# The largest expert goes last, and the final norm's steps are queued later beside it

## Chip, core and metric

The kernel runs on one core of one Trainium2 chip. The metric is the device time of one execution in microseconds, as the median of several runs. Engines are named as the profile names them: PE is TensorE, DVE is VectorE, ACT is ScalarE, POOL is GpSimd, SP is SyncE. Each engine works through its own instructions in the order in which they were queued.

## What is computed

One layer of a diffusion backbone over 1024 latent tokens of width 1024 with 256 context tokens: token mixers first, then a mixture of 16 experts, then an RMSNorm over the result. Only the last two matter here. Each token goes to two experts of one group, and each expert is a gated product of width 1536:

```python
def expert_block(args):
    xb, e = args
    return (jax.nn.silu(xb @ w_g[e]) * (xb @ w_u[e])) @ w_d[e]
...
y = y_blk[dest].reshape(n_tok, TOP_K, d) * weight[..., None].astype(h.dtype)
return jnp.sum(y, axis=1)
...
x = x + gt2 * y[:n_lat].reshape(bsz, seq, d)
...
return rms_norm(x, g_final)
```

## The kernel before

The last 1055 us or so of the span are a loop over 16 **slots**, one expert each. The order of the experts is a table of ranks by the number of their tokens: `RANK[slot]` is the rank of the expert that a slot works on (0 is expert 0, whose weights can be fetched before the counts are known; 1 is the largest of the others, 15 the smallest). `UNITS[slot]` follows from it: every expert has 128 token rows (the A rows, gathered into `xa`), rank 1 has two further **units** of 32 rows, ranks 2 to 9 have one, the others none (the B rows, gathered into `xb`; one unit is laid over the 128 partitions as four column quarters of 256). So there are slots of no unit, of one unit, and one of two units.

An expert's weights come in 18 **pages** of 1 MB, 12 of `w_gu` (gate and up) and 6 of `w_d` (down), which SP loads (`load`, L1179) into a ring of ten buffers named `raw` and `praw`. ACT copies a page to a rounded high part (`hl`, L1192), DVE subtracts it for a low part (L1193); three `hl` buffers exist. `block_a` (L1372) then makes 12 products of 128x512 for a page with the A rows, six for each column half (`pa`); `block_b` (L1385) uses the pages as they were loaded for the B rows (`pb`). A slot has three gate/up chunks of four pages (c0, c1, c2), whose results go through SiLU on ACT (`sa`, L1592; `sb_` for B rows), a product on DVE (L1593), and transposes on PE (`aat`, `abt`, copied to `aah`, `aal` and `abT`), and a down part of six pages, in two halves of three. With units, `block_b` of a chunk or a half comes ahead of its `block_a`. At a slot's end DVE scales the result (`ya`, L1632; `yb`, L1625) and POOL adds its rows to `x1_d` in DRAM by an indirect DMA (L1430).

The last slot also makes the final norm. `TAIL` says at which chunk which step is issued: `f0` to `f3` (`fetched`, L1510) read 256 rows of `x1_d` each, `f0` into a tile of its own (`fx`), the others into buffers of the page ring; `n0` to `n3` (`normed`) square 128 rows at a time with a running sum on ACT (`fq`, L1517), make 1/sqrt by 12 small DVE steps (`rstd`, L215 to L223), scale the rows by it and by g_final, and write them to `out` (L1525). `NE` says with which engine a half of such rows is scaled: "S" is a scaling on ACT (L1521) and a product on POOL (L1522), "V" one instruction on DVE (L1524). The rows of the last expert are written again behind that, from `xg`: the rows of `x1_d` gathered earlier plus `ya`, squared (L1635), normed (L1639), and scattered into `out` (L1534).

```python
TAIL = dict(g0=["f0", "f1"], g2=["g", "n0", "n1", "f2"], d0=["f3"], d2=["n2", "n3"])
RANK = (0, 1, 10, 2, 11, 3, 12, 4, 13, 5, 14, 6, 7, 8, 9, 15)
```

`g0` to `g2` are called behind c0 to c2, `d0` and `d2` behind a down page. The framework's scheduler queues an instruction where its own priorities put it, which can be ahead of the place at which it is written.

Of the kernel before, what the change touches and what calls it, by code (L numbers as in the profile page):

```python
# [21 lines left out]
E = 16  # L22
# [22 lines left out]
FQB = 1  # L45
EPX = 1
FOLD = 2
NE = ["SS", "SV", "SV", "VV"]
TAIL = dict(g0=["f0", "f1"], g2=["g", "n0", "n1", "f2"], d0=["f3"], d2=["n2", "n3"])
QW = 260  # L50


RANK = (0, 1, 10, 2, 11, 3, 12, 4, 13, 5, 14, 6, 7, 8, 9, 15)
UNITS = tuple(0 if r == 0 else 2 if r == 1 else 1 if r < 10 else 0 for r in RANK)
C_C, C_CC, C_G1, C_BB, C_BM, C_GLA, C_LNG = 0, 8, 16, 24, 40, 56, 64
N_COLS = 72
# [105 lines left out]
def body(tc, A, out):  # L162
# [1148 lines left out]
    def places():  # L1311

        X = mybir.AxisListType.X
        sq = [128, 16, 16]
        key = ep_.tile([128, 16], F32, name="key")
        V.scalar_tensor_tensor(key, cf, 16.0, ks[:, 3], op0=ALU.mult, op1=ALU.add)
        w = ep_.tile(sq, F32, name="w16")
        V.tensor_tensor(w, key[:, None, :].to_broadcast(sq), key[:, :, None].to_broadcast(sq), op=ALU.is_gt)
        rank = ep_.tile([128, 16], F32, name="rank")
        V.tensor_reduce(rank, w, axis=X, op=ALU.add)  # L1320
        sel = ep_.tile(sq, F32, name="sel")
        V.tensor_tensor(sel, ks[:, 0, :, None].to_broadcast(sq), rank[:, None, :].to_broadcast(sq), op=ALU.is_equal)
# [23 lines left out]
        V.tensor_reduce(rank[0:1, 0:1], more[:, 0], axis=X, op=ALU.max)  # L1346
        V.tensor_copy(cnt[:, 3:4], rank[0:1, 0:1])
# [15 lines left out]
        SP.dma_start(g2B[32 * g:32 * g + 32],  # L1363
                     mod_d[6 + g // 2:7 + g // 2, 256 * (g % 2):256 * (g % 2) + 256].to_broadcast([32, 256]))

    def block_a(acc, st, k0, pg, start, stop):

        wh, wl = pg
        for k in range(2):
            for n, (x, w) in enumerate(((0, wh), (0, wl), (1, wh))):  # L1370
                for h in range(2):
                    end = PE.matmul(acc[h], st[x][:, k0 + k, :], w[:, k, 512 * h:512 * h + 512],  # L1372
                                    start=start and (k, n) == (0, 0), stop=stop and (k, n) == (1, 2))
        return end

    def block_b(n, acc, st, k0, pgs, first, last):
# [127 lines left out]
    def rows_of(a, i):  # L1504
        return a[256 * i:256 * i + 256].rearrange("(j p) c -> p j c", j=2)

    def fetched(i, pool=None):

        fx[i] = (pool or ep_).tile([128, 2, D], F32, name="fx") if pool or i < EPX else page_tile([128, 2, D])
        GP.dma_start(fx[i], rows_of(x1_d, i))  # L1510

    def normed(i, gf):
        x1 = fx[i]
        sq = ep_.tile([128, D], BF16, name="fq", bufs=FQB)
        ss = ep_.tile([128, 2, 2], F32, name="fs", bufs=2)
        for j in range(2):
            SC.activation(sq, x1[:, j], AF.Square, accum_out=ss[:, 0, j:j + 1])  # L1517
        rstd(ss[:, 1], ss[:, 0], 2, 1.0 / D, ep_)
        for j in range(2):
            if NE[i][j] == "S":  # L1520
                SC.activation(x1[:, j], x1[:, j], AF.Copy, scale=ss[:, 1, j:j + 1])  # L1521
                GP.tensor_mul(x1[:, j], x1[:, j], gf)  # L1522
            else:
                V.scalar_tensor_tensor(x1[:, j], x1[:, j], ss[:, 1, j:j + 1], gf, op0=ALU.mult, op1=ALU.mult)  # L1524
        GP.dma_start(rows_of(out, i), x1)  # L1525

    def quarters(r0, tile_):
        a = A["rows"]
# [11 lines left out]
    def tail(at):  # L1540
        nonlocal gf, xg
        for n in TAIL.get(at, ()):
            if n == "g":
                gf = ep_.tile([128, D], F32, name="gf")
                bcast("rows", 2 * D, D, gf)
                xg = ep_.tile([128, D], F32, name="xg", tag="xa", bufs=1)
                gather(xg, x1_d, tkA[:, E - 1:E])
            elif n[0] == "f":
                fetched(int(n[1]))
            else:  # L1550
                normed(int(n[1]), gf)

    gf = xg = None
    wAB = prep_a(0, *first_xa, ch0), []
    before = []

# [13 lines left out]
    for e in range(E):  # L1570
        U = UNITS[e]
        left = None
        for c in range(3):
# [15 lines left out]
            for h in range(2):  # L1589
                sa = ep_.tile([128, 2, 128], F32, name="sa", bufs=4)  # L1590
                pv = pa[h].rearrange("p (g u n) -> p g u n", g=2, u=2)
                SC.activation(sa, pv[:, :, 0], AF.Silu)  # L1592
                mul = V.tensor_mul(sa, sa, pv[:, :, 1])  # L1593
                sas.append(sa)
            left = c, sas, sb_ if U else None, U
# [4 lines left out]
                    if e == 0:  # L1600
                        places()
            if e + 1 == E:
                tail(f"g{c}")
            elif c == 1:
                nxt = gathered(e + 1)
        pa, pb = [pt(f"pa{h}", "pa", 4) for h in range(2)], pt("pb", "pb", 2) if U else None
        for i in range(0, 6, 3):
# [4 lines left out]
            if i == 3 and e + 1 < E:  # L1612
                wAB = prep(e + 1, *nxt)
            for k in range(i, i + 3):
                end = block_a(pa, AA, 2 * k, page(), k == 0, k == 5)
                if k == 0 and not U:
                    turned_a(*left, end)
                if e + 1 == E and k % 2:
                    tail(f"d{k - 1}")
        ya = ep_.tile([128, D], F32, name="ya", bufs=2)  # L1620
        yb = ep_.tile([128, 2, 256], F32, name="yb", bufs=2)
        last = e + 1 == E
        wA, wB = wAB_
        for j in range(U):
            V.scalar_tensor_tensor(yb[:, j], pb[:, 256 * j:256 * j + 256], wB[j], g2B, op0=ALU.mult, op1=ALU.mult)  # L1625
        if last:

            sl = ep_.tile([128, 8], F32, name="sl")
            sq = ep_.tile([128, D], BF16, name="fq", bufs=FQB)
# [6 lines left out]
        if last:  # L1636
            V.tensor_add(sl[:, 6:7], sl[:, 4:5], sl[:, 5:6])
            rstd(sl[:, 7:8], sl[:, 6:7], 1, 1.0 / D, ep_)
            V.scalar_tensor_tensor(xg, xg, sl[:, 7:8], gf, op0=ALU.mult, op1=ALU.mult)  # L1639
            put_out(xg, tkA[:, e:e + 1], out, S - 1)  # L1640
        if last:
            break
        st = [put(ya, tkA[:, e:e + 1], x1_d, (), before)]
# [9 lines left out]
    any_more = nc.values_load(cnt[0:1, 3:4], min_val=0, max_val=1)  # L1653
    with tc.If(any_more > 0):
        put(ya, tkA[:, E - 1:E], x1_d)
        flat = more.rearrange("o b e -> o (b e)")
# [7 lines left out]
        np_ = tc.alloc_tile_pool(name="np", bufs=1)  # L1664
        for t in range(4):
            fetched(t, np_)
            normed(t, gf)
        np_.release()
    ep_.release()
# [17 lines left out]
```

## Time and profile before

| | |
|---|---|
| median of 3 runs (lowest to highest) | 2233.47 us (2231.7 to 2234.19) |
| the profiled execution | 2234.38 us, its span 2232.6 us |
| PE busy | 2152.0 us, 96% of the span |
| DVE, ACT, POOL busy | 63%, 47%, 10% |
| HBM | 236 GB/s over the span |

The span runs from the first to the last instruction in the profile of one execution, and the time holds 1.8 us more than it. Matmuls are pipelined, so a busy PE is only an engine that never waits for more than a moment. A busy share over the whole span says little about the last slot, which is 4% of it.

### The profile page before, as it was taken

The numbers are of one execution on the slowest core, as the hardware profiler recorded it, in microseconds if no ns is written. First come the engines' busy times: TensorE is split into PE (matmuls) and PEld (weight loads), VectorE is DVE, ScalarE is ACT, GpSimd is POOL, SyncE is SP. The second block draws the span as 40 slices with busy tenths as digits, with TensorE's granted clock in tenths as the row PEclk, the third lists the DMA queues.
The fourth block names the chain that finished last, engine by engine and source line by source line (L and its number), as shares of the span: only waits on it lengthen the run. The fifth ranks groups of instructions, "written<-read, shape, count | busy, mean of one in ns | idle before, by whom it ended". The sixth has DMA issues, their size and how long they took to land. (4 is left out here: it accounts for less than half of the span.)

```text
span 2232.6 us, 36046 instructions
## 1 busy us (share of the span) xinstructions
PE 2152.0 (96%) x14286; PEld 1788.1 (80%) x14287; DVE 1414.7 (63%) x2127; ACT 1057.8 (47%) x1327; POOL 212.6 (10%) x174
## 2 busy tenths in 40 slices
PE   8999999999999999999978999999999999999975
PEld 6999898888889978888966777787878787777753
DVE  5754214847672354344888568787978787777766
ACT  3412114635542234233226456676767666556554
POOL 0011000000000000000343111100101010100031
PEclk9999999999999999999989999999999999999988
DMA  7576433556652175545648779898989898877774
GB/s 297 180 226 178 157 131 105 178 186 198 219 201 72 38 258 202 191 135 205 189 185 304 269 261 368 301 368 306 364 301 377 302 350 337 290 277 295 283 245 160
DMA packets 141791, 529.63 MB, mean 237 GB/s; under 512 B 17126, under 2 KB 57758, under 8 KB 94512
## 3 DMA queue, kind: packets, MB, share of 16 engines
q1 hardware_dynamic: 119584, 467.84, 57.3%
q0 software_dynamic: 20880, 55.16, 8.6%
q10 hardware_dynamic: 1152, 4.26, 0.5%
q8 instruction: 114, 1.87, 0.3%
q14 instruction: 61, 0.50, 0.1%
HBM read 457.09 MB, written 70.31 MB: 236 GB/s over the span
## 5 line engine op out<-in xcount | busy, mean ns | idle before, releaser
L1193 DVE TENSOR_TENSOR hl<-praw,hl 128x2048 fp32r<-128x2048 f32 x174 | 400.3, 2303 | 130.5 <-ACT hl L1192 125.7
L1372 PE MATMUL pa<-hl,xah 128*128 128x512 f32 x1536 | 421.1, 395 | 19.8 <-ACT hl L1192 13.4
L1192 ACT ACTIVATE hl<-praw 128x2048 fp32r<-128x2048 f32 x174 | 333.6, 1919 | 151.7 <-PE pa L1372 150.5
L1372 PEld LDWEIGHTS pa<-hl,xah 128*128 128x128 f32 x1536 | 286.4, 189 | 85.2 <-ACT hl L1192 13.8
L1193 DVE TENSOR_TENSOR hl<-raw,hl 128x2048 fp32r<-128x2048 f32 x114 | 260.7, 2290 | 86.7 <-ACT hl L1192 83.1
L1192 ACT ACTIVATE hl<-raw 128x2048 fp32r<-128x2048 f32 x114 | 218.8, 1919 | 100.3 <-PE pa L1372 95.5
L1372 PE MATMUL pa<-hl,xal 128*128 128x512 f32 x768 | 238.2, 391 | 0.0
L256 PE MATMUL mm<-wh,hxh 128*128 128x256 f32 (+1 forms) x768 | 218.9, 285 | 1.0 <-DVE vv L285 0.7
L1372 PE MATMUL pa<-hl,aah 128*128 128x512 f32 x768 | 212.4, 398 | 6.5 <-DVE hl L1193 5.0
L256 PE MATMUL mm<-wl,hxh 128*128 128x256 f32 (+1 forms) x768 | 217.7, 283 | 0.0
L256 PE MATMUL mm<-wh,hxl 128*128 128x256 f32 (+1 forms) x768 | 217.3, 283 | 0.0
L256 PE MATMUL mm<-hxh,wh 128*128 128x512 f32 x448 | 176.4, 394 | 0.0
L256 PE MATMUL mm<-hxh,wl 128*128 128x512 f32 x448 | 176.3, 394 | 0.0
L256 PE MATMUL mm<-hxl,wh 128*128 128x512 f32 x448 | 176.3, 393 | 0.0
L1372 PEld LDWEIGHTS pa<-hl,aah 128*128 128x128 f32 x768 | 142.8, 190 | 35.6 <-DVE hl L1193 5.9
L1372 PEld LDWEIGHTS pa<-hl,xal 128*128 128x128 f32 x768 | 145.0, 189 | 31.1
L256 PEld LDWEIGHTS mm<-wh,hxh 128*128 128x128 f32 x768 | 146.5, 191 | 1.8 <-DVE vv L285 0.9
L256 PEld LDWEIGHTS mm<-wl,hxh 128*128 128x128 f32 x768 | 146.6, 191 | 0.0
L238 DVE TENSOR_TENSOR wl<-wraw,wh 128x2048 fp32r<-128x2048 f32 (+1 forms) x36 | 82.7, 2298 | 100.7 <-ACT wh L237 100.6
L256 PEld LDWEIGHTS mm<-wh,hxl 128*128 128x128 f32 x768 | 146.3, 190 | 0.0
L1372 PE MATMUL pa<-hl,aal 128*128 128x512 f32 x384 | 120.2, 393 | 0.0
L237 ACT ACTIVATE wh<-wraw 128x2048 fp32r<-128x2048 f32 (+1 forms) x36 | 69.0, 1918 | 65.9 <-PE mm L256 60.7
(489 smaller groups left out, 3588.2 us busy)
## 6 DMA issues: line engine op xcount, KB each, us to landing
praw<-in_w_gu_dram SPq DMA_DIRECT2D x116, 1024.0 KB, 6.2
raw<-in_w_gu_dram SPq DMA_DIRECT2D x76, 1024.0 KB, 6.3
praw<-in_w_d_dram SPq DMA_DIRECT2D x58, 1024.0 KB, 7.2
raw<-in_w_d_dram SPq DMA_DIRECT2D x38, 1024.0 KB, 7.0
wraw<-in_w_in_dram SPq DMA_DIRECT2D x24, 1024.0 KB, 4.7
wraw<-in_w_mod_dram SPq DMA_DIRECT2D x18, 1024.0 KB, 5.9
vb<-v_d POOLq DMA_DIRECT2D x16, 1024.0 KB, 6.8
xt<-in_x_dram SPq DMA_DIRECT2D x16, 512.0 KB, 5.5
```

Of the source, the lines that this page charges most:

```text
L237: SC.activation(wh[:, :n], raw[:, :n], AF.Copy)
L238: V.tensor_sub(wl[:, :n], raw[:, :n], wh[:, :n].bitcast(F32))
L256: end = PE.matmul(acc, Wst[a](k), Wmv[b](k), start=n == 0, stop=n == tot - 1)
L1192: SC.activation(hl[:, 0, :], raw, AF.Copy)
L1193: V.tensor_sub(hl[:, 1, :], raw, hl[:, 0, :].bitcast(F32))
L1372: end = PE.matmul(acc[h], st[x][:, k0 + k, :], w[:, k, 512 * h:512 * h + 512], start=start and (k, n) == (0, 0), stop=stop and (k, n) == ( ...
```

## The change

- `RANK` puts the largest expert (two units) into slot 15 and the smallest into slot 12. Slot 1 now has one unit. The list of units by slot changes from 0 2 0 1 0 1 0 1 0 1 0 1 1 1 1 0 to 0 1 0 1 0 1 0 1 0 1 0 1 0 1 1 2.
- `TAIL` fetches `f0` and `f1` behind c0, and `f2` and `f3` behind c1; `n0` is issued behind c1 and `n2` behind c2. `normed` now takes four times 128 rows at once (two fetches), squares them on ACT, runs one `rstd` for four columns, and scales all of them on DVE; nothing of it is left on POOL but the DMAs. `issue_after` holds its instructions back until the chunk's SiLU and product have been queued.
- The units of the last expert are normed beside the down part: `xq` (their rows of `x1_d`), squares, a product `sums` with the constant `k32` on PE which adds the four quarters of a row, an `rstd`, and two scatters into `out`.
- `block_a` of the very last page makes all products of the first column half, then those of the second.

```diff
-NE = ["SS", "SV", "SV", "VV"]
-TAIL = dict(g0=["f0", "f1"], g2=["g", "n0", "n1", "f2"], d0=["f3"], d2=["n2", "n3"])
+TAIL = dict(g0=["f0", "f1"], g1=["g", "f2", "f3", "n0"], g2=["n2"])
...
-RANK = (0, 1, 10, 2, 11, 3, 12, 4, 13, 5, 14, 6, 7, 8, 9, 15)
+RANK = (0, 2, 10, 3, 11, 4, 12, 5, 13, 6, 14, 7, 15, 8, 9, 1)
...
-        for k in range(2):
-            for n, (x, w) in enumerate(((0, wh), (0, wl), (1, wh))):
-                for h in range(2):
+        steps = [(h, k, n) for k in range(2) for n in range(3) for h in range(2)]
+        for h, k, n in sorted(steps) if in_turn else steps:
...
     def normed(i, gf):
+        ss = ep_.tile([128, 2, 4], F32, name="fs", bufs=2)
+        tiles = [fx[i + n // 2][:, n % 2] for n in range(4)]
+        for n, x1 in enumerate(tiles):
+            SC.activation(sq, x1, AF.Square, accum_out=ss[:, 0, n:n + 1])
+        rstd(ss[:, 1], ss[:, 0], 4, 1.0 / D, ep_)
+        for n, x1 in enumerate(tiles):
+            V.scalar_tensor_tensor(x1, x1, ss[:, 1, n:n + 1], gf, op0=ALU.mult, op1=ALU.mult)
+            if n % 2:
+                GP.dma_start(rows_of(out, i + n // 2), fx[i + n // 2])
...
+                with tc.issue_after(act.ins), tc.issue_after(mul.ins):
+                    normed(int(n[1]), gf)
...
+            if i == 3 and last:
+                sl = ep_.tile([128, 16], F32, name="sl")
+                sq = ep_.tile([128, D], BF16, name="fq", bufs=FQB)
+                for j in range(U):
+                    V.scalar_tensor_tensor(yb[:, j], pb[:, 256 * j:256 * j + 256], wB[j], g2B, op0=ALU.mult,
+                                           op1=ALU.mult)
+                    V.tensor_add(xq[:, j], xq[:, j], yb[:, j])
+                    SC.activation(sq[:, 256 * j:256 * j + 256], xq[:, j], AF.Square, accum_out=sl[:, 8 + j:9 + j])
             for k in range(i, i + 3):
-                end = block_a(pa, AA, 2 * k, page(), k == 0, k == 5)
+                end = block_a(pa, AA, 2 * k, page(), k == 0, k == 5, last and k == 5)
...
+                if last and k == 4:
+                    p = pt("sums", "pt", 2)
+                    with tc.issue_after(end.ins):
+                        PE.matmul(p[:, 0:U], k32, sl[:, 8:8 + U], start=True, stop=True)
+                    rstd(sl[:, 10:10 + U], p[:, 0:U], U, 1.0 / D, ep_)
+                    ends = []
+                    for j in range(U):
+                        V.scalar_tensor_tensor(xq[:, j], xq[:, j], sl[:, 10 + j:11 + j], gq, op0=ALU.mult,
+                                               op1=ALU.mult)
+                        ends.append(put_out(xq[:, j], tkB[:, j, e:e + 1], out_quarter, 4 * S - 1, ends))
```

How the queues stand now is seen best in the instructions' order. On ACT, in the last slot, before the change, from the splits of c0's last pages on (`hl` a page's split, `sa` SiLU, `fq` the norm's squares, `fx` the norm's rows):

```order
L1192 ACTIVATE hl<-raw 128x2048 x2
L1592 ACTIVATE sa<-pa_18881 128x256
L1592 ACTIVATE sa<-pa_18882 128x256
L1517 ACTIVATE fq,fs<-fx 128x1024 x2
L1192 ACTIVATE hl<-raw 128x2048
L1521 ACTIVATE fx<-fx,fs 128x1024 x2
L1192 ACTIVATE hl<-praw 128x2048
```

The same engine and slot after the change, from the SiLU of c1 on:

```order
L1600 ACTIVATE sa<-pa_18712 128x256
L1600 ACTIVATE sa<-pa_18713 128x256
L1518 ACTIVATE fq,fs<-fx 128x1024
L1191 ACTIVATE hl<-raw 128x2048
L1518 ACTIVATE fq,fs<-fx 128x1024
L1518 ACTIVATE fq,fs<-raw 128x1024 x2
L1594 ACTIVATE sb__19060<-pb 128x256
L1426 ACTIVATE aah<-aat 128x512
```

The first squares stood behind c0's SiLU, ahead of the split of c1's first page; now they stand behind c1's SiLU, with four squares for the two before.

On SP, the last loads of down pages before the change, with the counters each waits for (DMASW counts DMAs that POOL queued, DMAHW those of SP and ACT):

```order
L1179 DMA raw_19185<-in_w_d_dram 128x2048 [waits DMAHW1_49,DVE_49]
L1179 DMA raw_19209<-in_w_d_dram 128x2048 [waits DMASW6_49,DMASW1_49,DMAHW2_49,DVE_49,Pool_49]
L1179 DMA praw_19228<-in_w_d_dram 128x2048 [waits DMAHW3_49,Activation_49]
L1179 DMA praw_19245<-in_w_d_dram 128x2048 [waits DMAHW4_49,Activation_49]
L1179 DMA praw_19307<-in_w_d_dram 128x2048 [waits DMAHW5_49,Activation_49]
```

And after it:

```order
L1178 DMA raw_19101<-in_w_d_dram 128x2048 [waits DMAHW3_49,DVE_49,PE_49]
L1178 DMA praw_19103<-in_w_d_dram 128x2048 [waits DMAHW7_49]
L1178 DMA praw_19105<-in_w_d_dram 128x2048 [waits DMAHW0_49]
L1178 DMA praw_19212<-in_w_d_dram 128x2048 [waits DMAHW1_49]
L1178 DMA praw_19214<-in_w_d_dram 128x2048 [waits DMAHW0_49,DMAHW2_49,DVE_49,PE_49]
```

The second down page took the buffer of `f1` and waited for the write of its rows to `out` (DMASW); now no page load of the last slot waits for a DMA of POOL.

On DVE, the end of the last slot before the change (`ya` the scaled result of a column half, `xg` the rows to be normed):

```order
L1632 SCALAR_TENSOR_TENSOR ya<-pa_19183,wA,g2A 128x512
L1632 SCALAR_TENSOR_TENSOR ya<-pa_19184,wA,g2A 128x512
L1634 TENSOR_TENSOR xg<-xg,ya 128x512 x2
L1637 TENSOR_TENSOR sl<-sl 128x1
L215 TENSOR_SCALAR rs_m<-sl 128x1
```

And after it (`xq` and `gq` belong to the units):

```order
L1654 SCALAR_TENSOR_TENSOR ya<-pa_19096,wA,g2A 128x512
L222 SCALAR_TENSOR_TENSOR rs_y<-rs_t,rs_y 128x2
L1656 TENSOR_TENSOR xg<-xg,ya 128x512
L220 TENSOR_TENSOR rs_t<-rs_y 128x2
L1654 SCALAR_TENSOR_TENSOR ya<-pa_19097,wA,g2A 128x512
L221 SCALAR_TENSOR_TENSOR rs_t<-rs_t,rs_m 128x2
L1656 TENSOR_TENSOR xg<-xg,ya 128x512
L222 SCALAR_TENSOR_TENSOR sl<-rs_t,rs_y 128x2
L1647 SCALAR_TENSOR_TENSOR xq<-xq,sl,gq 128x256 x2
L1659 TENSOR_TENSOR sl<-sl 128x1
```

The halves' steps now alternate, with steps of the units' `rstd` and their scaling in between.

## Rows read from the trace of the kernel before

**Rows 1.** Windows: slots 0, 1, 2, 3, 11 and 15, and the end behind PE.

```profile
core 0: us, PE busy (x) PEld busy (x) DVE busy (x) ACT busy (x) POOL busy (x), PEclk, DMA share, GB/s
1176.96:1238.03 61.07, 56.55 (x244) 44.89 (x243) 49.30 (x68) 39.27 (x31) 14.78 (x3) 0.95 0.80 309
1238.03:1322.86 84.83, 84.83 (x821) 61.58 (x821) 50.32 (x43) 41.03 (x35) 10.09 (x5) 1.00 0.71 247
1322.86:1374.76 51.90, 51.90 (x239) 42.47 (x238) 47.69 (x34) 38.88 (x30) 5.72 (x2) 1.00 0.99 383
1374.76:1443.34 68.58, 68.58 (x528) 51.51 (x528) 48.76 (x40) 40.41 (x35) 6.77 (x4) 1.00 0.82 297
1856.63:1925.80 69.17, 69.14 (x531) 51.44 (x530) 48.88 (x40) 40.78 (x36) 6.96 (x4) 1.00 0.80 295
2132.71:2215.03 82.32, 57.79 (x229) 44.38 (x227) 60.17 (x83) 46.42 (x45) 23.52 (x14) 0.85 0.64 230
2215.03:2232.60 17.57, 0.01 (x1) 0.00 (x0) 5.77 (x18) 1.33 (x4) 1.05 (x1) 0.56 0.06 21
```

**Rows 2.** Timeline of slot 15's first wait (start, duration, engine, work, [idle before]).

```profile
2147.56 0.81 POOL L1510 DMA_DIRECT2D fx<-x_d  x1 [8.16 <-DMA x_d<-ya,tks]
...
2153.00 1.06 ACT L1517 ACTIVATE fq<-fx 128x1024 bf16<-128x1024 f32 x1 [8.78 <-DMA fx<-x_d]
...
2155.24 1.89 ACT L1192 ACTIVATE hl<-raw 128x2048 fp32r<-128x2048 f32 x1
...
2157.18 1.22 PE L1372 MATMUL pa<-hl,xah 128*128 128x512 f32 x2 [13.43 <-ACT hl L1192]
```

**Rows 3.** Waits of PE in slot 15 (us in total, times, longest).

```profile
PE pa L1372 <- ACT hl L1192: 14.9, 2, 13.4
PE pa L1372 <- DVE hl L1193: 9.7, 5, 5.0
```

**Rows 4.** Windows within slot 15, columns as in Rows 1.

```profile
2184.12:2194.25 10.13, 8.69 (x38) 6.72 (x39) 9.89 (x24) 7.58 (x10) 1.76 (x1) 1.00 0.82 321
...
2200.01:2204.90 4.89, 4.89 (x14) 3.92 (x15) 4.89 (x3) 0.67 (x1) 0.00 (x0) 0.65 0.82 300
```

**Rows 5.** Waits of SP's queue from slot 1 on (us, times, longest).

```profile
SPq L1179 <- DMA out_dram<-raw: 25.6, 1, 25.6
```

**Rows 6.** Timeline of slot 1: c1's SiLU, c2's last page, second down half.

```profile
1274.80 0.66 ACT L1592 ACTIVATE sa<-pa 128x256 f32<-128x256 f32 x2 [0.57 <-PE pa L1372]
...
1275.35 1.91 ACT L1192 ACTIVATE hl<-praw 128x2048 fp32r<-128x2048 f32 x1
...
1283.52 0.69 DVE L1427 TENSOR_TENSOR aal<-aat,aah 128x512 fp32r<-128x512 f32 x1 [0.35 <-ACT aah L1426]
...
1287.79 2.29 DVE L1193 TENSOR_TENSOR hl<-praw,hl 128x2048 fp32r<-128x2048 f32 x1 [3.58 <-ACT hl L1192]
...
1290.63 0.62 PE L1372 MATMUL pa<-hl,xal 128*128 128x512 f32 x2
1291.08 1.07 PE L1372 MATMUL pa<-hl,xah 128*128 128x512 f32 x4
...
1308.42 5.39 PE L1385 MATMUL pb<-raw,abT 128*32 128x256 f32 x96
```

**Rows 7.** Source line L1524: ns shortest/median/longest, first and last start.

```profile
L1524 DVE SCALAR_TENSOR_TENSOR raw<-raw,fs,gf x2: 1287/2024/2762, 2178.5 to 2191.2; 128x1024 f32<-128x1024 f32 x2
L1524 DVE SCALAR_TENSOR_TENSOR praw<-praw,fs,gf x2: 1280/1283/1286, 2195.9 to 2204.3; 128x1024 f32<-128x1024 f32 x2
```

**Rows 8.** Timeline of POOL beside the slower L1524, and of the end.

```profile
2176.99 3.18 POOL L1522 TENSOR_TENSOR raw<-raw,gf 128x1024 f32<-128x1024 f32 x1 [7.93 <-ACT raw L1521]
...
2218.26 0.16 DVE L1637 TENSOR_TENSOR sl<-sl 128x1 f32<-128x1 f32 x1 [0.80 <-ACT fq L1635]
...
2220.77 1.28 DVE L1639 SCALAR_TENSOR_TENSOR xg<-xg,sl,gf 128x1024 f32<-128x1024 f32 x1
2222.34 1.05 POOL L1534 DMA_INDIRECT out_dram<-xg,tks  x1 [15.76 <-DVEq L1654]
```

More of the change, by code (lines that the diff above doesn't have):

```diff
@@ L1364, in body, with block_a @@
                      mod_d[6 + g // 2:7 + g // 2, 256 * (g % 2):256 * (g % 2) + 256].to_broadcast([32, 256]))
-    def block_a(acc, st, k0, pg, start, stop):
+    def block_a(acc, st, k0, pg, start, stop, in_turn=False):
         wh, wl = pg
-        for k in range(2):
-            for n, (x, w) in enumerate(((0, wh), (0, wl), (1, wh))):
-                for h in range(2):
-                    end = PE.matmul(acc[h], st[x][:, k0 + k, :], w[:, k, 512 * h:512 * h + 512],
-                                    start=start and (k, n) == (0, 0), stop=stop and (k, n) == (1, 2))
+        steps = [(h, k, n) for k in range(2) for n in range(3) for h in range(2)]
+        for h, k, n in sorted(steps) if in_turn else steps:
+            x, w = ((0, wh), (0, wl), (1, wh))[n]
+            end = PE.matmul(acc[h], st[x][:, k0 + k, :], w[:, k, 512 * h:512 * h + 512],
+                            start=start and (k, n) == (0, 0), stop=stop and (k, n) == (1, 2))
         return end
@@ L1507, in fetched @@
     def fetched(i, pool=None):
-        fx[i] = (pool or ep_).tile([128, 2, D], F32, name="fx") if pool or i < EPX else page_tile([128, 2, D])
+        fx[i] = (pool or ep_).tile([128, 2, D], F32, name="fx", bufs=2 if pool else 1) if pool or i < EPX else page_tile([128, 2, D])
         GP.dma_start(fx[i], rows_of(x1_d, i))
     def normed(i, gf):
-        x1 = fx[i]
         sq = ep_.tile([128, D], BF16, name="fq", bufs=FQB)
[L1515 to L1525, printed above, removed]
+        ss = ep_.tile([128, 2, 4], F32, name="fs", bufs=2)
[7 more added lines that the diff above has]
+                GP.dma_start(rows_of(out, i + n // 2), fx[i + n // 2])
     def quarters(r0, tile_):
@@ L1538, in put_out, with tail @@
         return st
-    def tail(at):
-        nonlocal gf, xg
+    def tail(at, act, mul):
+        nonlocal gf, gq, xg, xq, k32
         for n in TAIL.get(at, ()):
@@ L1547, in tail @@
                 gather(xg, x1_d, tkA[:, E - 1:E])
+                gq = ep_.tile([128, 256], F32, name="gq", tag="sel")
+                quarters(2 * D, gq)
+                k32 = ep_.tile([128, 128], F32, name="k32")
+                SP.dma_start(k32, A["k32"])
+                xq = ep_.tile([128, 2, 256], F32, name="xq", tag="xb", bufs=1)
+                for j in range(UNITS[E - 1]):
+                    gather(xq[:, j], x1_quarter, tkB[:, j, E - 1:E])
             elif n[0] == "f":
@@ L1550, in tail @@
             else:
-                normed(int(n[1]), gf)
-    gf = xg = None
+                with tc.issue_after(act.ins), tc.issue_after(mul.ins):
+                    normed(int(n[1]), gf)
+    gf = gq = xg = xq = k32 = None
+    out_quarter = out.rearrange("t (g c) -> (t g) c", g=4)
     wAB = prep_a(0, *first_xa, ch0), []
@@ L1591, in body @@
                 pv = pa[h].rearrange("p (g u n) -> p g u n", g=2, u=2)
-                SC.activation(sa, pv[:, :, 0], AF.Silu)
+                act = SC.activation(sa, pv[:, :, 0], AF.Silu)
                 mul = V.tensor_mul(sa, sa, pv[:, :, 1])
@@ L1602, in body @@
             if e + 1 == E:
-                tail(f"g{c}")
+                tail(f"g{c}", act, mul)
             elif c == 1:
@@ L1606, in body @@
         pa, pb = [pt(f"pa{h}", "pa", 4) for h in range(2)], pt("pb", "pb", 2) if U else None
+        last = e + 1 == E
+        wA, wB = wAB_
+        ya = ep_.tile([128, D], F32, name="ya", bufs=2)
+        yb = ep_.tile([128, 2, 256], F32, name="yb", bufs=2)
         for i in range(0, 6, 3):
@@ L1611, in body @@
                     turned_a(*left, end)
-            if i == 3 and e + 1 < E:
+            if i == 3 and not last:
                 wAB = prep(e + 1, *nxt)
+            if i == 3 and last:
[6 more added lines that the diff above has]
+                    SC.activation(sq[:, 256 * j:256 * j + 256], xq[:, j], AF.Square, accum_out=sl[:, 8 + j:9 + j])
             for k in range(i, i + 3):
-                end = block_a(pa, AA, 2 * k, page(), k == 0, k == 5)
+                end = block_a(pa, AA, 2 * k, page(), k == 0, k == 5, last and k == 5)
                 if k == 0 and not U:
                     turned_a(*left, end)
[L1618 to L1624, printed above, removed]
+                if last and k == 4:
[8 more added lines that the diff above has]
+                        ends.append(put_out(xq[:, j], tkB[:, j, e:e + 1], out_quarter, 4 * S - 1, ends))
+        for j in range(0 if last else U):
             V.scalar_tensor_tensor(yb[:, j], pb[:, 256 * j:256 * j + 256], wB[j], g2B, op0=ALU.mult, op1=ALU.mult)
-        if last:
-            sl = ep_.tile([128, 8], F32, name="sl")
-            sq = ep_.tile([128, D], BF16, name="fq", bufs=FQB)
         for h in range(2):
@@ L1639, in body @@
             V.scalar_tensor_tensor(xg, xg, sl[:, 7:8], gf, op0=ALU.mult, op1=ALU.mult)
-            put_out(xg, tkA[:, e:e + 1], out, S - 1)
+            put_out(xg, tkA[:, e:e + 1], out, S - 1, ends)
         if last:
@@ L1655, in body @@
         put(ya, tkA[:, E - 1:E], x1_d)
+        for j in range(UNITS[E - 1]):
+            put(yb[:, j], tkB[:, j, E - 1:E], x1_quarter)
         flat = more.rearrange("o b e -> o (b e)")
@@ L1663, in body @@
                     overflow_block(at_, b, row)
-        np_ = tc.alloc_tile_pool(name="np", bufs=1)
-        for t in range(4):
-            fetched(t, np_)
+        np_ = tc.alloc_tile_pool(name="np", bufs=2)
+        for t in range(0, 4, 2):
+            for i in range(t, t + 2):
+                fetched(i, np_)
             normed(t, gf)
```

2 lines of the change are left out of this document (1 added, 1 removed).

## Prediction

> **What bounds the kernel now.** I read the windows by slot first, since the loop over experts is half of the span and its slots repeat. A slot of one unit lasts 68.58 us ahead of a slot without units and 69.17 us ahead of one with units, a slot without units 51.90 us, the slot of two units 84.83 us; in each of them PE is busy for the whole window at a granted clock of 1.00 [rows 1]. So from slot 1 to slot 14 PE alone sets the pace: splits, loads and the rest lie beside its products. Slots 0 and 15 differ. Slot 0 has 4.5 us without PE, which the change does not touch. Slot 15 has no units, so at the pace of its kind it would last 51.90 us, and it lasts 82.32 us with 57.79 us of PE [rows 1]. That is 30.42 us lost in one slot.
>
> The timeline of slot 15 says to what. ACT stood idle for 8.78 us on the norm's first square, whose rows (`fx`) had not landed; the split of c1's first page was queued behind it, began at 2155.24, and PE waited 13.43 us for it [rows 2]. The list of waits gives all of them: 14.9 us for ACT's split in two waits, 9.7 us for DVE's in five, the longest 13.4 and 5.0 us [rows 3]. The 5.0 us have another origin: SP waited 25.6 us until the normed rows of `f1` had been written to `out`, before it could load a down page into their buffer, and the last five pages came late [rows 5]. The waits make 24.6 us; most of the rest is the lower clock behind the long ones: a mean of 0.65, between the two levels of 1.2 and 2.4 GHz, in the window that follows the 5.0 us wait [rows 4]. Behind the last product 17.57 us remain: the last rows' norm, their scatter and the program's end [rows 1].
>
> **The change, part by part.**
>
> The order of the experts. The same 16 experts do the same products, so the total of PE's work stays. Slot 0 keeps its 61.07 us: its pages and its expert are the same. Then come six pairs of a slot of one unit and one without, 68.58 + 51.90 = 120.48 us each; slots 13 and 14, of one unit and each ahead of a slot with units, 69.17 us each; and slot 15 with two units, 84.83 us if nothing stands in PE's way. From 1176.96, the start of slot 0: 1176.96 + 61.07 + 6 x 120.48 + 2 x 69.17 + 84.83 = 2184.08 us for PE's end, before new waits [rows 1].
>
> The first wait. With two units, c0 and c1 have to pass before the norm's first square is queued. In slot 1, the template for the new slot 15, c1's SiLU ends at 1275.46, 37.4 us behind the slot's start [rows 1, 6]. In the old slot 15 the fetch of `fx` was issued 14.9 us behind the start and the square could run 20.3 us behind it [rows 1, 2]. So the rows are there 17 us early, and the ACT wait is gone.
>
> The waits of the page loads. By the order no load of the last expert waits for a DMA of POOL, so the 25.6 us go [rows 5]. The ring has three buffers less while the norm's rows are held, though, and the fifth down page now takes the third one's buffer. In the template the second half's products with raw pages begin at 1308.42, three pages of products behind the moment at which the third page was split [rows 6]. I count nothing for it; the nearest row for a late load is the 5.0 us wait [rows 3].
>
> The norm's work, first round. It hides beside PE as long as the splits stay ahead. From the template: SiLU ends at 1275.46 on ACT. Then four squares and one page split stand in its queue; two squares took from 2153.00 to 2155.24 [rows 2], so 2 x 2.24 + 1.91 = 6.4 us, to 1281.9. DVE makes 12 small steps, 2.5 us (2218.26 to 2220.77, with one more step) [rows 8], four scalings of 1.28 us [rows 7], and a subtraction for the transposed chunk of 0.7 us: to 1290.2 [rows 6]. Only then comes the low part of c2's last page, 2.29 us, to 1292.5. PE reaches this page at 1291.08 and wants the low part two products later; two products take from 1290.63 to 1291.08, so at 1291.53 [rows 6]. So PE waits about **0.9 us**, where the template, done at 1287.79 + 2.29 = 1290.08, had 1.45 us to spare. A wait of this size did not lower the clock: in the window from 2184.12 to 2194.25 PE lost 1.44 us and kept 1.00 [rows 4].
>
> The second round starts behind c2's SiLU and has more cover: the first down half's raw products, its transposes, its three pages and the second half's raw products. A page is twelve products, 2.72 us, so c2 ends at 1291.08 + 2.72 = 1293.8 and its SiLU at 1294.5; 6.4, 2.5, 5.1 and 0.7 us, and 2.29 us for the fourth down page's low part, lead to 1311.5. PE wants that at 1308.42 + 5.39 + 0.45 = 1314.3 [rows 6]: 2.8 us of margin, no wait. Two more low parts, four steps of some 0.4 us and the units' squares end at about 1319; PE reaches `sums` two pages behind 1313.8, at 1319.2. I count nothing there.
>
> For the scaling I take 1.28 us and not the 2.76 us that one of the four took [rows 7]: the long one began at 2178.5, beside a product on POOL from 2176.99 on [rows 8], the two of 1.28 us ran beside none, and the change leaves POOL no product. At 2.76 us a round is 5.9 us longer: 6.8 us of wait in the first, 3.1 in the second (5.9 less 2.8 of margin), and 2.6 at `sums` (1319 + 5.9 against 1319.2 + 3.1), 12.5 in all for the 0.9, and the time would be 2215.
>
> The Trainium skill, page SBUF — State Buffer, section Who interferes with whom, has a rule for this: a DVE instruction with two SBUF inputs is blocked by a GpSimd instruction that reads SBUF, for the whole of it, but not by one that only writes. By that rule the scalings run at their short duration and the time is 2203; by the long row it is 2215. The trace agrees as far as it goes [rows 7, 8]; no row shows a scaling beside a DMA issue.
>
> The end. The last page's first half is complete six products (1.36 us) earlier, so one scaling, one addition and one square of the A rows leave the end. But DVE does the units' steps there: between the two halves stand three small steps, behind them the last one and two scalings of 256 columns. DVE's queue has then as much behind the last product as it had, and I leave the 17.57 us as they are; between 1.3 us less and 0.6 us more is possible. The two scatters of the units stand ahead of the last one on POOL, which was idle for 15.76 us there [rows 8].
>
> Sum: 2184.08 + 0.9 + 17.57 = 2202.6 against a span that ends at 2232.6 [rows 1]: **30.0 us** less. The profiled execution took 2234.38 us, 0.9 more than the median of the runs, so from the median: 2233.47 - 30.0 = **2203 us**.
>
> **The rivals.**
>
> *The norm's work becomes a wait* (0.14). It lies in c2 and in the down part of slot 15, at DVE. It happens if scalings are slow, or squares wait, or a wait is long enough for the clock to fall. For it: DVE has only 1.45 us of margin in the template. Against it: POOL has no product left. From 2207 (half of it) to 2215.
>
> *Everything hides* (0.09): no wait in c2, the end gains its 1.3 us, and the transposes for a next expert, which are in the 84.83 us, drop out. 2199 to 2200.5.
>
> *The change doesn't do what it says* (0.03): the fetches come too late again, because they stand behind something on POOL or wait for a ring buffer, and ACT stalls as before. They would have to lose the 17 us of lead and then some; the time would stay near 2233.
>
> *Slower, by the loads* (0.04). In a slot without units the DMA engines are busy for 0.99 of the time at 383 GB/s, and in the old slot 1 for 0.71 [rows 1]. Slot 1 was the long rest before the first such slot; now it has 16 us less. If the ring doesn't fill up in 68.58 us, PE waits in slot 2, and if a pair of 120.48 us then never lets it recover, in all six pairs. From 5 us a pair the gain is gone; at 7 us the time is 2245. Against it: the old slots 3 to 10 were such pairs in a row, and in the windows of a slot without units and of one with one unit PE is busy throughout, the DMA engines at 0.82 in the latter [rows 1].
>
> **How the numbers follow.** The forecast has 0.68, with its own range from 2200.5 to 2206; 0.02 is left for what I haven't seen. From 2199 to 2213 lie the forecast, the case in which all hides, and most of the first rival: more than 8 in 10. Some 0.2% (4.5 us) is what a measurement here can tell from no change. Faster has all of the first three cases and the unseen rest, 0.93; same 0.03; slower 0.04.
>
> **What the profile after would show.** Right: windows of the pairs at 68.58 and 51.90 us with PE busy throughout; a slot 15 of 85 to 87 us, with one wait of PE for DVE's `hl` in c2 of about a microsecond and a clock of 1.00; squares without idle ACT ahead of them; no wait of SP for `out_dram`; eight scalings of 1.28 us; an end of 17 to 18 us. Wrong: a PE wait in slot 2, scalings near 2.8 us, a clock below 1.00 in slot 15, or down pages whose loads begin behind the first half.

## The result and the profile after

The changed kernel takes 2202.44 us (median of 4 runs, 2202.24 to 2207.76) against 2232.72 us for the kernel before (4 runs): a ratio of 0.9871, with an interval from 0.9859 to 0.9884. The profiled execution took 2202.61 us, 31.8 us less than the profiled one of before.

The windows of the changed kernel by slot (0, 1, 2, 13, 14, 15, and the end behind PE), columns as in [rows 1] and to be read beside them:

```profile
1175.83:1236.98 61.15, 56.71 (x240) 44.47 (x239) 49.20 (x68) 38.93 (x31) 12.08 (x2) 0.94 0.81 306
1236.98:1305.56 68.58, 68.58 (x528) 51.57 (x528) 48.76 (x40) 40.38 (x35) 6.98 (x4) 1.00 0.83 306
1305.56:1357.44 51.88, 51.88 (x240) 42.50 (x238) 47.66 (x34) 38.87 (x30) 5.76 (x2) 1.00 0.98 385
...
1959.74:2028.94 69.20, 69.17 (x530) 51.47 (x529) 48.88 (x40) 40.78 (x36) 6.96 (x4) 1.00 0.81 296
2028.94:2098.56 69.62, 69.60 (x534) 51.87 (x533) 49.11 (x40) 41.09 (x37) 7.92 (x5) 1.00 0.74 263
2098.56:2183.66 85.10, 84.96 (x816) 60.97 (x815) 61.94 (x84) 45.52 (x51) 14.27 (x12) 1.00 0.64 239
2183.66:2200.90 17.24, 0.00 (x1) 0.00 (x0) 5.82 (x22) 1.45 (x4) 3.06 (x3) 0.58 0.11 43
```

Every slot shown now has the length of its kind to 0.5 us. The last one, with two units and the whole norm beside it, lasts 85.10 us, and PE is busy for 84.96 of them at a granted clock of 1.00; the last slot of before was 30.42 us longer than its kind. DVE does the norm's steps there (61.94 us busy, as against 50.32 in the old slot of two units) at next to no cost to PE. The list of PE's waits from slot 1 to the last product is empty.

The timeline of the last slot's first round, ACT, DVE, POOL and PE, beside [rows 2] and [rows 6]:

```profile
2135.56 0.66 ACT L1600 ACTIVATE sa<-pa 128x256 f32<-128x256 f32 x2 [0.57 <-PE pa L1372]
2136.10 1.06 ACT L1518 ACTIVATE fq<-fx 128x1024 bf16<-128x1024 f32 x1
...
2142.48 0.17 DVE L214 TENSOR_SCALAR rs_m<-fs 128x4 f32<-128x4 f32 x1 [1.11 <-ACT fq L1518]
...
2144.86 2.48 DVE L1521 SCALAR_TENSOR_TENSOR fx<-fx,fs,gf 128x1024 f32<-128x1024 f32 x2
2147.26 2.48 DVE L1521 SCALAR_TENSOR_TENSOR raw<-raw,fs,gf 128x1024 f32<-128x1024 f32 x2
2147.64 0.76 POOL L1523 DMA_DIRECT2D out_dram<-fx  x1 [22.42 <-DVE fx L1521]
2149.65 0.69 DVE L1427 TENSOR_TENSOR aal<-aat,aah 128x512 fp32r<-128x512 f32 x1
2150.26 2.28 DVE L1192 TENSOR_TENSOR hl<-raw,hl 128x2048 fp32r<-128x2048 f32 x1
...
2151.84 1.48 PE L1372 MATMUL pa<-hl,xah 128*128 128x512 f32 x4
```

The square begins behind the SiLU with no idle time ahead of it, where ACT stood idle for 8.78 us before [rows 2]. Behind the scalings comes the low part of c2's last page, and PE's group of four products takes 1.48 us where such a group takes 1.07 [rows 6]: 0.4 us, the one delay by the norm that shows in PE's rows.

Of SP's waits from slot 1 on the one for `out_dram` [rows 5] is gone. A load of a down page now waits for an earlier one:

```profile
SPq L1178 <- DMA praw<-in_w_d_dram: 8.5, 1, 8.5
```

The end, by POOL and DVE behind PE's last product at 2183.66:

```profile
2182.32 0.75 DVE L1654 SCALAR_TENSOR_TENSOR ya<-pa,wA,g2A 128x512 f32<-128x512 f32 x1
...
2186.24 0.16 DVE L1659 TENSOR_TENSOR sl<-sl 128x1 f32<-128x1 f32 x1
...
2190.33 0.98 POOL L1532 DMA_INDIRECT out_dram<-xg,tks  x1 [1.73 <-DVEq L1676]
```

The scaling of the first half's result (`ya`) begins 1.3 us ahead of the end of the last product. The sum of the two halves' squares (`sl`) follows the last product by 2.58 us, 2186.24 - 2183.66, against 3.23 us before, 2218.26 - 2215.03 [rows 8]; the last scatter by 6.67 us against 7.31.

### The profile page after: what moved, and what is told of

It reads as the page before. It is cut to its first block, busy times and chain, and to the rows that moved or that the text cites. A ratio compares the mean times of both kernels' runs of the same rounds, so it can differ in the third digit from the quotient of the medians.

```text
span 2200.9 us, 36059 instructions
## 1 busy us (share of the span) xinstructions
PE 2146.6 (98%) x14288; PEld 1786.6 (81%) x14289; DVE 1413.5 (64%) x2123; ACT 1054.0 (48%) x1327; POOL 201.7 (9%) x172
## 5 line engine op out<-in xcount | busy, mean ns | idle before, releaser
L1192 DVE TENSOR_TENSOR hl<-praw,hl 128x2048 fp32r<-128x2048 f32 x173 | 395.8, 2291 | 119.9 <-ACT hl L1191 114.5
```

Source lines behind the costliest of these rows:

```text
L1192: V.tensor_sub(hl[:, 1, :], raw, hl[:, 0, :].bitcast(F32))
```

## Experiments

No experiment changes the work ahead of the slots, yet slot 0 began at times from 1173 to 1182 us in the profiles. The runs were taken on two chips, where the kernel before took 2231.9 to 2240.6 us and 2229.9 to 2238.0 us. Each ratio is to the kernel before on the same chip; medians of different kernels differ by this scatter too. So the length of the last slot and of the end, from one profile each, is read beside the medians.

**The order alone** (with the units' own norm, which comes with it). The edit also puts back the old body of `normed` and its calls behind the down pages (at the first `...` and behind the last line).

```
-TAIL = dict(g0=["f0", "f1"], g1=["g", "f2", "f3", "n0"], g2=["n2"])
+NE = ["SS", "SV", "SV", "VV"]
+TAIL = dict(g0=["f0", "f1"], g2=["g", "n0", "n1", "f2"], d0=["f3"], d2=["n2", "n3"])
...
-                with tc.issue_after(act.ins), tc.issue_after(mul.ins):
-                    normed(int(n[1]), gf)
+                normed(int(n[1]), gf)
...
-                end = block_a(pa, AA, 2 * k, page(), k == 0, k == 5, last and k == 5)
+                end = block_a(pa, AA, 2 * k, page(), k == 0, k == 5)
```

> The changed kernel with the norm's steps put back as they were before: the old table of steps, rounds of two tiles, the four scalings that go by ACT and POOL, no holding back behind c1's and c2's SiLU, and alternating halves on the last page. The order of the experts and the units' own norm stay as changed. Theory: the order carries nearly all of the gain, since with two units ahead of c1 the rows land (some 24 us behind the slot's start) before their squares are due; ACT's wait is gone. What stays are the wait of a page load for rows being written to out (up to 5 us of PE in the kernel before), some clock behind it (1.7 us at 0.65 over 4.9 us) and a norm whose last rows are queued late, up to 8 us in the end. 2203 to 2217 us, PE waiting for ACT's split in the last slot under 2 us. Rival: the queueing carries it; then ACT's idle 8 us or so ahead of a square and PE's wait of more than 10 us return, and the time is 2225 or more.

2230.88 us, a ratio of 0.9985 to the kernel before (0.9973 to 0.9996), above the 2203 to 2217 of the theory. The theory falls: the order by itself brings next to nothing. Windows of the last slot and of the end:

```profile
2097.38:2192.69 95.31, 86.96 (x816) 62.45 (x815) 54.99 (x67) 43.55 (x46) 21.86 (x13) 0.96 0.51 180
2192.69:2228.05 35.36, 0.00 (x1) 0.00 (x0) 14.89 (x59) 7.08 (x13) 6.85 (x6) 0.53 0.20 80
```

Waits of PE and of SP's queue in the last slot (us in total, times, longest):

```profile
PE aat L1572 <- DVE sa L1603: 6.7, 1, 6.7
PE pa L1373 <- DVE hl L1193: 1.6, 1, 1.6
...
SPq L1179 <- DMA out_dram<-raw: 28.5, 1, 28.5
```

ACT's timeline, the first square and the first one of the last rounds:

```profile
2119.91 1.06 ACT L1518 ACTIVATE fq<-fx 128x1024 bf16<-128x1024 f32 x1 [10.51 <-DMA fx<-x_d]
...
2195.96 1.06 ACT L1518 ACTIVATE fq<-raw 128x1024 bf16<-128x1024 f32 x1
```

ACT stands idle for 10.5 us on the square's rows again, from 12 us behind the slot's start on, because the scheduler had queued the square ahead of splits of c1's pages and even of c0's SiLU; two units in the slot do not move it. PE waits 8.3 us, 6.7 of them for c0's result. A page load waits 28.5 us for rows written to `out`, as in [rows 5]. And the norm's last rounds are queued behind everything: their squares begin 3.3 us behind the last product, and the end lasts 35.36 us instead of 17.24. Slot and end together are 28.3 us longer than in the changed kernel, nearly all that the change gains.

**The hold alone undone.**

```
-                with tc.issue_after(act.ins), tc.issue_after(mul.ins):
-                    normed(int(n[1]), gf)
+                normed(int(n[1]), gf)
```

> The changed kernel with one thing undone: the norm's steps are no longer held back behind the SiLU of their chunk, and stand where the scheduler puts them. On ACT the first two squares then stand some 12 us behind the start of the last slot, as in the kernel that had the order alone, where ACT stood idle for 10.5 us on the rows and PE waited 6.7 us behind it. Theory: holding the steps back takes that wait away, not the order; without it the wait is back and the last slot is 6 to 9 us longer: 2209 to 2212 us. Rival: the wait of the kernel with the order alone came from its other differences (rounds of two, work on POOL); then it is 2202 to 2204 us.

2216.18 us, 0.9930 (0.9908 to 0.9952), above the 2209 to 2212 expected. The window of the last slot:

```profile
2097.03:2194.48 97.45, 88.50 (x816) 62.97 (x815) 61.77 (x84) 45.16 (x51) 15.07 (x12) 0.95 0.57 209
```

Waits of ACT and of PE in it:

```profile
ACT fq L1518 <- DMA fx<-x_d: 10.9, 1, 10.9
...
PE aat L1569 <- DVE sa L1600: 7.1, 1, 7.1
PE pa L1372 <- DVE hl L1192: 1.8, 1, 1.8
```

So it is the hold. The slot is 12.35 us longer (97.45 against 85.10), more than the 6 to 9 expected: 8.9 us of waits, and 3.5 us more of busy PE (88.50 against 84.96), at a mean clock of 0.95. The end has its 17.3 us, so the 18 us more in the end of the order-alone kernel belong to the old steps (their table, their rounds and the halves), not to the missing hold. That makes three parts and not two. Slot and end together last 130.7 us with the order alone, 114.8 with the new steps and no hold, and 102.3 in the changed kernel: next to the order, the new steps bring 15.9 us and the hold 12.4. What the table, the rounds and the move of the scalings from POOL to DVE bring one by one was not tried.

**The queueing alone.**

```
-RANK = (0, 2, 10, 3, 11, 4, 12, 5, 13, 6, 14, 7, 15, 8, 9, 1)
+RANK = (0, 1, 10, 2, 11, 3, 12, 4, 13, 5, 14, 6, 7, 8, 9, 15)
```

The units' product `sums` and its `rstd` are left out as well, since this last slot has no units.

> The changed kernel with the old order of the experts: the last slot has no units, all the rest of the norm stays as changed (squares behind c1's SiLU and behind c2's, rounds of four tiles, all scalings on DVE). Theory: the two units are the cover. ACT's wait of 13 us goes, but DVE splits pages for 2.29 of every 2.72 us there, and the norm's two rounds of 7.6 us (12 small steps of 2.5 us, four scalings of 1.28 us) find only some 6 us of slack behind c1: PE waits 8 to 12 us for DVE's split, and the clock falls behind a part of it. 2212 to 2222 us. Rival: the queueing is enough by itself, and the order only hides what was hidden: 2202 to 2206 us.

2215.41 us, 0.9917 (0.9898 to 0.9935), in the range of the theory. The window of the last slot:

```profile
2128.53:2193.71 65.18, 55.52 (x229) 43.72 (x227) 54.87 (x62) 41.56 (x41) 10.63 (x9) 0.92 0.74 275
```

PE's waits in it:

```profile
PE pa L1372 <- DVE hl L1192: 7.3, 3, 4.7
PE pa L1372 <- ACT hl L1191: 2.3, 1, 2.3
```

ACT's timeline, the first square:

```profile
2157.17 1.06 ACT L1518 ACTIVATE fq<-fx 128x1024 bf16<-128x1024 f32 x1
```

ACT does not stand idle ahead of the square here either. The slot is 13.3 us longer than the 51.88 us of its kind, where the slot of before lost 30.4. PE waits 7.3 us for DVE's splits, just under the 8 to 12 expected, and 2.3 us for ACT's. The order is needed too, but for the other half of the loss: it gives DVE time for the norm.

**How much cover.** The experts of ranks 1 and 2 are exchanged, so that an expert of one unit is last:

```
-RANK = (0, 2, 10, 3, 11, 4, 12, 5, 13, 6, 14, 7, 15, 8, 9, 1)
+RANK = (0, 1, 10, 3, 11, 4, 12, 5, 13, 6, 14, 7, 15, 8, 9, 2)
```

> The changed kernel with the experts of ranks 1 and 2 exchanged: the largest, with two units, in slot 1 and an expert of one unit last. Theory: cover is counted in raw products. One unit less takes 3.25 us of PE from ahead of c2's pages and 6.5 us from the down part, (84.83 - 68.58) / 5 for each of the five groups. With 0.4 us of PE wait now in c2 and 2.8 us of margin in the second round that makes 3.7 us and 3.7 us of PE wait, and 2209.5 us (2206 to 2213). Rival: one unit is cover enough, since the split pages stand ready in buffers: 2201.5 to 2204 us.

2207.84 us, 0.9874 (0.9857 to 0.9890). The window of the last slot:

```profile
2121.00:2193.97 72.97, 71.43 (x522) 49.60 (x521) 59.31 (x74) 43.85 (x49) 13.83 (x11) 1.00 0.74 276
```

PE's timeline in c1 of it, and the only wait that its list names:

```profile
2136.69 0.73 PE L1372 MATMUL pa<-hl,xah 128*128 128x512 f32 x2
2137.36 1.07 PE L1385 MATMUL pb<-praw,xbT 128*32 128x256 f32 x16
...
2188.42 0.73 PE L1372 MATMUL pa<-hl,aah 128*128 128x512 f32 x2 [1.54 <-DVE hl L1192]
```

The slot is 3.8 us longer than the 69.20 us of slot 13 in the changed kernel, which has one unit too: half of the 7.4 us of the theory. Only 1.5 us of it are a wait for DVE. The other 2.3 us are busy time of PE at a clock of 1.00 (71.43 us against 69.17), and the list of waits doesn't say where they come from. The timeline has raw products (`pb`) between those with split pages, where my count took them as one block ahead; whether this makes the waits shorter and the busy time longer was not tried by itself. So one unit does not hide the norm, but missing cover is shown for 1.5 us only. The times alone would not tell: the median is 5.4 us above the changed kernel's, with a scatter of 7 us between this kernel's runs, and the ratios to the kernel before are 0.9874 and 0.9871.

**The norm taken out.**

```
-TAIL = dict(g0=["f0", "f1"], g1=["g", "f2", "f3", "n0"], g2=["n2"])
+TAIL = dict(g0=["f0", "f1"], g1=["g", "f2", "f3"])
```

> The changed kernel without the two rounds of the norm (no squares, no small steps, no scalings, no writes of those rows, which the output then lacks); the rows are still read into the ring's buffers, and the last expert's own rows are normed as before. Theory: all of the norm but 0.4 us of PE's wait in c2 lies beside PE: 2202.0 us, 0.2 to 0.8 less than the changed kernel. Rival: the norm still costs in the last slot by late loads or in the end, and 2 us or more go: 2200.5 us or less.

2202.41 us, 0.9857 (0.9839 to 0.9874); the times can't tell it from the changed kernel. The windows of the last slot and of the end:

```profile
2097.04:2181.71 84.67, 84.67 (x816) 60.98 (x815) 49.24 (x52) 36.78 (x35) 11.35 (x8) 1.00 0.50 191
2181.71:2198.64 16.93, 0.00 (x0) 0.00 (x0) 5.80 (x22) 1.44 (x4) 3.02 (x3) 0.64 0.11 44
```

The slot is 0.43 us shorter, 84.67 against 85.10, and the end 0.3 us. That is all that the norm of 1024 rows still costs there; what is left in this slot is PE's own work, 84.67 us busy out of 84.67.

**The margins of DVE.**

```
             V.scalar_tensor_tensor(x1, x1, ss[:, 1, n:n + 1], gf, op0=ALU.mult, op1=ALU.mult)
+            V.scalar_tensor_tensor(x1, x1, ss[:, 1, n:n + 1], gf, op0=ALU.mult, op1=ALU.mult)
```

> The changed kernel with each of the norm's eight scalings on DVE made twice (those rows are scaled twice in the output). Theory by the margins of the prediction: each round gets 4 x 1.28 = 5.1 us longer; the first has 0.4 us of PE wait already and so gives 5.5, the second has 2.8 us of margin and gives 2.3, `sums` some 0.7: the last slot 8.1 us longer, 2210.5 us (2208 to 2213 with a lower clock behind the longer wait). Rival: DVE's slack is wider than the margins say, and under 3 us come: 2202.5 to 2205 us.

2210.90 us, 0.9897 (0.9878 to 0.9916). The window of the last slot:

```profile
2098.07:2191.65 93.58, 87.45 (x816) 62.10 (x815) 71.52 (x92) 45.18 (x51) 14.26 (x12) 0.98 0.58 217
```

PE's timeline at its two waits:

```profile
2153.88 1.46 PE L1385 MATMUL pb<-praw,abT 128*32 128x256 f32 x18
2156.90 0.73 PE L1372 MATMUL pa<-hl,xah 128*128 128x512 f32 x2 [1.57 <-DVE hl L1192]
...
2184.52 0.94 PE L1372 MATMUL pa<-hl,aah 128*128 128x512 f32 x2 [4.56 <-DVE hl L1192]
```

The slot is 8.5 us longer, against 8.1 from the margins (whose parts, 5.5, 2.3 and 0.7, make 8.5); 10.2 us of scalings were added. That the sums agree is partly luck, for the parts don't: 1.6 us of wait in the first round (5.5 expected), 4.6 us in the second (2.3), none listed at `sums` (0.7). The waits make 6.1 us; the other 2.5 us are more busy time of PE (87.45 against 84.96) at a mean clock of 0.98, which the margins did not include. PE has 50 raw products of the down part queued ahead of c2's last products here (the last 18 of them are the first line shown), which cover a part of the first wait and no longer stand behind c2 as cover for the second round. That this explains the two sizes is read from the timeline and was not tried by itself.

**Work on POOL beside the scalings.**

```
-            SC.activation(sq, x1, AF.Square, accum_out=ss[:, 0, n:n + 1])
+            done = SC.activation(sq, x1, AF.Square, accum_out=ss[:, 0, n:n + 1])
+        if not big:
+            pz = ep_.tile([128, 256], F32, name="pz", tag="w16")
+            for n in range(14):
+                g = GP.tensor_mul(pz, gf[:, 0:256], gf[:, 256:512]) if i == 0 else GP.memset(pz, 0.0)
+                tc.add_manual_dep(g.ins, done.ins.name, SYNC, reason="beside the scalings")
...
```

> The changed kernel with idle work for POOL beside the norm's scalings: in the first round 14 products of 128x256 (two inputs read), in the second 14 memsets of 128x256 (nothing read), both released by the round's last square; the output stays. Theory: POOL's products were what made one scaling of the kernel before 2.76 us long; the four of the first round take 2.0 us or more each, the four of the second stay at 1.28. PE waits 3 to 6 us more in c2 and the time is 2205.5 to 2208.5 us. Rival 1: POOL is not the cause; all eight stay at 1.28 and the time at 2202.5. Rival 2: any work on POOL is; all eight are long and the time is 2209 or more.

2209.64 us, 0.9894 (0.9876 to 0.9911), above the 2205.5 to 2208.5 of the theory. The window of the last slot:

```profile
2098.12:2190.16 92.04, 87.33 (x816) 62.22 (x815) 67.40 (x84) 45.62 (x51) 38.26 (x40) 0.96 0.59 221
```

The scalings by source line, columns as in [rows 7]:

```profile
L1526 DVE SCALAR_TENSOR_TENSOR praw<-praw,fs,gf x4: 1279/1280/1285, 2171.1 to 2174.6; 128x1024 f32<-128x1024 f32 x4
...
L1526 DVE SCALAR_TENSOR_TENSOR fx<-fx,fs,gf x2: 1761/1802/1843, 2147.0 to 2148.8; 128x1024 f32<-128x1024 f32 x2
L1526 DVE SCALAR_TENSOR_TENSOR raw<-raw,fs,gf x2: 1742/1750/1758, 2150.4 to 2152.1; 128x1024 f32<-128x1024 f32 x2
```

The timeline, DVE's small steps beside the products, PE's wait, and POOL's memsets:

```profile
2142.04 0.17 DVE L214 TENSOR_SCALAR rs_m<-fs 128x4 f32<-128x4 f32 x1 [1.11 <-ACT fq L1518]
2142.25 0.60 DVE L217 TENSOR_SCALAR rs_t<-rs_m 128x4 int32<-128x4 int32 x1
2142.88 0.17 DVE L218 TENSOR_SCALAR rs_y<-rs_t 128x4 int32<-128x4 int32 x1
...
2156.72 1.22 PE L1372 MATMUL pa<-hl,xah 128*128 128x512 f32 x2 [4.71 <-DVE hl L1192]
...
2168.43 5.12 POOL L1522 MEMSET pz<- 128x256 f32 x14 [4.21 <-ACT fq L1518]
```

Beside POOL's products each scaling takes 1.74 to 1.84 us, and six of the first round's twelve small steps 0.6 instead of 0.17; beside the memsets (2168.43 to 2173.55, so the first two of that round's scalings) the scalings stay at 1.28. For the scalings POOL's products are the cause, and not any work on POOL. The size was expected too long (2.0 or more): each scaling lost some 0.5 us, less than one product of 128x256 takes (0.72), where the 2.76 us stood beside a product of 3.18 us [rows 7, 8]. PE's wait in c2, 4.7 us, lies in the range of the theory all the same, because the small steps, which the theory had left out, got longer too. They take 5.0 us here, from 2142.04 to the first scaling at 2147.0, against 2.4 us in the changed kernel, 2144.86 - 2142.48: they lose some 2.6 us, and the four scalings some 2.0. The slot is 6.9 us longer: this wait and 2.4 us more busy time of PE (87.33 against 84.96), at a mean clock of 0.96.

**The halves of the last page.**

```
-                end = block_a(pa, AA, 2 * k, page(), k == 0, k == 5, last and k == 5)
+                end = block_a(pa, AA, 2 * k, page(), k == 0, k == 5)
```

> The changed kernel with the last page's products in the old order, the two column halves alternating. Theory: the halves in turn give next to nothing, since DVE has the units' steps to do there: the end behind the last product 17.2 to 17.9 us, the time 0 to 0.7 us above the changed kernel, 2202.4 to 2203.1. Rival: the first half's steps did leave the end, and undoing it costs the full 1.4 us of six products: an end of 18.6 us and 2203.8.

2204.80 us (5 runs, 2202.39 to 2210.90), 0.9874 (0.9855 to 0.9894): the medians can't tell. The profile can, in the end's window:

```profile
2184.61:2203.06 18.45, 0.00 (x1) 0.00 (x0) 6.36 (x20) 1.33 (x4) 4.21 (x3) 0.57 0.11 40
```

DVE's timeline there:

```profile
2184.22 0.88 DVE L1647 SCALAR_TENSOR_TENSOR xq<-xq,sl,gq 128x256 f32<-128x256 f32 x2
2185.02 1.41 DVE L1654 SCALAR_TENSOR_TENSOR ya<-pa,wA,g2A 128x512 f32<-128x512 f32 x2
...
2188.47 0.16 DVE L1659 TENSOR_TENSOR sl<-sl 128x1 f32<-128x1 f32 x1 [0.85 <-ACT fq L1657]
```

`sl` follows the last product by 3.86 us, 2188.47 - 2184.61, against 2.58 in the changed kernel: 1.28 us, and the end is 1.2 us longer. The rival has it. The same profile shows what the units cost in the end. DVE's timeline of the kernel before:

```profile
2214.85 1.41 DVE L1632 SCALAR_TENSOR_TENSOR ya<-pa,wA,g2A 128x512 f32<-128x512 f32 x2 [3.69 <-PE pa L1372]
```

There `ya` began 0.18 us ahead of the last product's end, 2215.03 - 2214.85; here it begins 0.41 us behind it, 2185.02 - 2184.61, since the units' scalings stand ahead of it on DVE. That is 0.6 of the 0.9 us by which this end, 18.45 us, is longer than the 17.57 us of before.

## Why the prediction was right, point by point

*The order, 2184.08.* Together with the 0.9 us of wait it is right to 0.2 us, counted from the start of slot 0. PE ended at 2183.66 against 2184.98 = 2184.08 + 0.9. Of the 1.3 us, 1.13 lie ahead of slot 0, which began at 1175.83 instead of 1176.96, where nothing was changed; that part is scatter that no step of the sum covers. From there the pairs lasted 68.58 + 51.88 or so each, slot 14 0.45 us more than counted (69.62 for 69.17), slot 15 0.63 less than 84.83 + 0.9. Without the norm's rounds slot 15 lasts 84.67 us, so the 84.83 taken from slot 1 served.

*The first wait.* Gone, as said, but the prediction gave the reason loosely. "With two units, c0 and c1 have to pass before the norm's first square is queued" is true of the changed kernel by its hold, not by its units. The kernel with order and rounds and no hold kept ACT idle for 10.9 us; the one with the hold and no units had no wait of ACT for the rows. The theory that I put to the test first, that the order carries nearly all, fell with it.

*The page loads, 0.* Right: no wait for `out_dram`, and the 8.5 us that SP waited for an earlier page cost PE nothing.

*The first round, 0.9 us.* The mechanism is right, at the place named; the size is half, 0.43 us by the kernel without the norm. The chain from the SiLU to the low part took 16.4 us (2136.10 to 2152.54) where I had 17.0: scalings of 1.28 us follow each other at 1.20, and the small steps took 2.4 us, not 2.5. That a wait of this size does not lower the clock was read from a window that ends with its wait of 1.44 us [rows 4], so it could not show what comes behind it. The runs do: the clock was 1.00 over the whole last slot of the changed kernel, and of the one with one unit last, with its wait of 1.54 us.

*The second round and `sums`, 0.* Right. The last of the units' squares was done 2.1 us ahead of `sums`, where I had counted 0.2.

*Scalings at 1.28 us.* Right, all eight (1.279 to 1.285 us in the profile), and the reason is now shown and not only argued from one row: POOL's products lengthen them, to 1.74 to 1.84 us; memsets don't, nor do DMA issues (the one at 2147.64 stands beside scalings of 1.28 us). The Trainium skill, page SBUF — State Buffer, section Who interferes with whom, says of a DVE instruction with two SBUF inputs that it contends with a GpSimd instruction that reads SBUF, and not with one that only writes it. The trace agrees, with 1.74 to 1.84 us beside products that read and 1.28 beside memsets.

*The end, unchanged.* The sum is nearly right, 17.24 for 17.57, and so is the balance behind it, that the first half's steps leave the end and the units' steps take their place. The runs give the sizes: the halves in turn take 1.2 us off the end, and without them the end with units is 18.45 us, 0.9 more than the end of before. What fell is the reading that I took from the balance before the run with alternating halves, that the halves in turn give next to nothing: without them the units' steps still stand in the end.

*The rivals.* A slot without units behind slot 1 was no danger: slot 2 lasted 51.88 us with PE busy throughout at a DMA share of 0.98. The rival in which the norm's work becomes a wait shows its price where its condition is made: 6.9 us with POOL's products beside the first round, 8.5 with the scalings doubled. Its lower bound, 2207, is called half of the price; half of the 12.5 us on a time without any wait, 2233.47 - 30.0 - 0.9 = 2202.6, would be 2209, which changes neither the forecast nor a chance.

## What to carry to other kernels

Moving a stage beside a longer one does not by itself hide it: look at where the queue of each engine puts its instructions. An in-order engine that meets an instruction whose data has not landed holds up all behind it, so hold such work back until its rows are there. Then see to it that the engine that waits for the work has enough other work queued ahead, as cover. Here the last slot lost 30.4 us before. With the new steps it lost 13.3 us with the hold and no cover, 12.8 with the cover and no hold (97.45 against 84.67), and 0.4 with both. Look behind the last product too: with the old steps and the new order the end was 18.1 us longer.

## What was not expected of the hardware

A lock-step of DVE and POOL: beside a row of POOL products of 128x256 (0.72 us and more each), DVE's steps of 128x4 took 0.17 and 0.6 us in turn, and POOL's products, 0.74 us beside these short steps, took 1.6 us beside the scalings and up to 2.73 us beside DVE's splits. It looks as if each engine waited for about one instruction of the other at a time, which I read from these durations and did not try by itself. Among the steps that waited is `rs_t<-rs_m` (L217), which has a single tensor as input. And at the first memset, which begins at 2168.43, one small step of DVE with a single tensor as input (L218, at 2168.45) took 0.31 us instead of 0.17, though the scalings beside memsets lost nothing.
